# First down projection of a decoder trunk on one Trainium2 core: nine pairs of inner tiles as block products and four plain tiles

## The chip, the cores and the metric

The kernel is one program on one core of a Trainium2 chip. The metric is the device time of one execution, in microseconds (us). Names used below: PE (TensorE, the matmuls) and PEld (its weight loads), DVE (VectorE), ACT (ScalarE), POOL (GpSimd) and SP (SyncE). POOL and SP start DMAs here, each in the order of its own instruction stream; an instruction of any engine that waits for a semaphore holds up all that stands behind it on that engine. "Landing" is the moment at which a DMA's semaphore tells that its data are there.

## The reference, cut to what matters

The reference is one decoder layer on x of 512 x 1024, in float32, with a SwiGLU before and one behind a mixer:

```python
def swiglu(x, w_gate, w_up, w_down):
    return (jax.nn.silu(x @ w_gate) * (x @ w_up)) @ w_down
...
    x = x + 0.5 * swiglu(rmsnorm(x, ffn1_norm[l]), ffn1_wg[l], ffn1_wu[l], ffn1_wd[l])
    x = x + hybrid_mixer(...)
    x = x + 0.5 * swiglu(rmsnorm(x, ffn2_norm[l]), ffn2_wg[l], ffn2_wu[l], ffn2_wd[l])
```

The change is in the last product of the first line, h @ ffn1_wd: h is 512 x 2816 and ffn1_wd is 2816 x 1024. The inner size of 2816 makes 22 inner tiles of 128.

## The kernel before, in words

Every float32 product is made of three matmuls on rounded parts (fp32r): each operand is split into a rounded part and a remainder, and high x high, high x remainder and remainder x high are summed in PSUM. The rounding of a weight tile is an ACT instruction (`wh<-...`), its remainder a DVE subtraction (`wl<-...`, which reads `wh`). The function wsplit (line 242) does both.

**Stage U, the first up projection** (ffn_up, line 426, called at line 1082 with w1u) makes the 22 tiles of h; its last stretch is a stream of steps (p, w), block products of the weights of tile pair w, w from 0 to 15. Per w, three partial sums of weights are needed. They are kept in SBUF tiles: s1 and s3 are loaded by SP and completed by a POOL DMA that adds a second block as it lands (accum_op=ALU.add); s2 is made by DVE (s1 plus a block) and, for most w, turned into s4 by one more POOL DMA that adds the block a12 into the same tile. In the trace all of these POOL DMAs read `s<-w1u`. The last step of the stream is (3, 15): it uses the s4 of w = 15.

**Stage D, the first down projection** (block_down, line 821, with plain = PLAIN1 and pairs = PAIRS1) takes the 22 tiles of h in two ways:

- A plain tile k has two steps ("D", half, k), one for each half of the 1024 output columns. Each step is 4 x 3 matmuls of 512 columns. Its h tile is split into hh and hl (function halve, during stage U).
- A pair j of inner tiles, a(j) and b(j), has seven steps (p, j), p = 1 to 7: block products in place of the eight block multiplications of a plain 2 x 2 scheme (Strassen's scheme, in a form with few additions). Each step is 4 x 3 matmuls of 256 columns. The seven weight operands are a11, a12, a22 and the sums s1 = a21 + a22, s2 = s1 + a11, s3 = a11 + a21 (with the signs of the scheme held by the other side) and s4 = s2 + a12. The seven moving operands are tiles cm of 128 x 512, a rounded half and a remainder half, made of a(j), b(j) and differences of them: `cr<-h,h` and `h<-h` are the two DVE subtractions of function differences (line 882), and operand (line 900) makes the rounded half on ACT and the remainder on DVE (or, for p = 4, by a POOL DMA).

The order of work in stage D is a list, `steps`. Before, it is 6 plain steps of half 0; then p = 1, 2, 5 for all j; then p = 6 and 3, with four plain steps of half 1 among them; then p = 7; two plain steps; and p = 4: 68 steps. What each step needs is hung on a table of tasks by step number (function task), and the tasks of step i are issued right after the matmuls of step i: the split of step i's weights at i - 4, most operands at i - 5 or i - 6, the differences of pair j at step j, the operand of (7, j) at j + 1. Tasks with negative numbers are issued in the last steps of stage U (parameter ahead of ffn_up), in program order behind what that step issued itself. A finished chain of products is added into x by four DVE instructions (results1, `x<-aux,x` after the plain steps of half 0, `x<-mm,x` after p = 1).

The sums s1, s2 and s4 of a pair are made one after the other in one SBUF tile, sums[j] (trace name `sm`; there are eight such tiles, two buffers of 2048 columns), by an SP load and three POOL DMAs with addition, while the steps that use the earlier sum run. s3 is made beforehand in a DRAM tensor, `kept` (trace name `scr`), by two POOL DMAs (lines 976 and 977), and is loaded by SP thirteen steps ahead of its use.

The weights of a step are split into a third of a rotating set of buffers: wh and wl have three buffers of 1024 columns (tile pool wsp), so two steps share one, and the splits run at most six steps ahead of PE.

The class Blocks (line 322) exists already for the second feed-forward layer: it owns four DRAM tensors for one pair's s1 to s4, and stages() returns six groups of DMAs, in which each group needs the landing of the one before: SP copies a21 into s1 and s3; POOL adds a22 and a11 to them; POOL copies s1 into s2; adds a11; copies s2 into s4; adds a12.

Of the kernel before, what the change touches and what calls it, by code (L numbers as in the profile page):

```python
# [9 lines left out]
F32 = mybir.dt.float32  # L10
# [4 lines left out]
P = 128  # L15
S = 512
D = 1024
# [25 lines left out]
HS = S // 2  # L43
TAIL2 = 4
LEAD = 4
PLAIN1, PAIRS1, PAIRS2, TAIL = 6, 8, 11, 3
DIRECT1, DIRECT2 = 4, 4
SUMS_AHEAD = 3
UNITS, SUMS_FROM, SUMS_PART, DIRECT_PART, SUMS_STEPS, SUMS_TIME = 6, 37, 0.93, 0.04, 44, 142
# [130 lines left out]
def hybrid_kernel(ctx, tc, xt, vec, w1u, w1d, wm, wki, wrg, watt, wrnn, wout, w2u, w2d, gf, out):  # L180
# [4 lines left out]
    Q = plan.engine("SP", nc.sync)  # L185
# [17 lines left out]
    def nm(s):  # L203
        cnt[0] += 1
        return f"{s}_{cnt[0]}"

    def slot(dt=F32, name="s"):
        return plan.take("slot", big.tile([P, S], dt, tag="slot", name=nm(name)))
# [612 lines left out]
    def block_down(hs, wd, sums, plain, pairs, blocks=None):  # L821
# [7 lines left out]
        steps = [("D", 0, k) for k in range(plain)] + [(p, j) for p in (1, 2, 5) for j in range(pairs)]  # L829
        for p in (6, 3):  # L830
            for j in range(pairs):
                steps += [(p, j)] + [("D", 1, (6, 3).index(p) * 2 + j // 3)] * (j in (2, 5) and plain > 2)
        steps += [(7, j) for j in range(pairs)] + [("D", 1, k) for k in range(plain - 2, plain)] + [(4, j) for j in range(pairs)]
        if blocks:
            steps = [(p, j) for p in (1, 2, 6, 5, 7, 3, 4) for j in range(pairs)]
# [3 lines left out]
        def task(i, *fs):  # L839
            tasks.setdefault(i, []).extend(fs)  # L840

        def block(b, j):

            i, half = b * (pairs // 2) + j // 2, j % 2 * S
            return wd[i][:, half:half + S]

        units, turned, ra, raws, s3 = {}, {}, {}, {}, {}

        def source(i):
            p, j = steps[i]  # L850
            b = blocks[j]
            return {1: b.a11, 2: b.a12, 3: b.s4, 4: b.a22, 5: b.s1, 6: b.s2, 7: b.s3}[p]

        def load_pair(i):
            raws[i] = raw.tile([P, WMAX], F32, tag="raw", name=nm("wr"))
            for n in range(min(2, len(steps) - i)):
                Q.dma_start(raws[i][:, n * S:(n + 1) * S], source(i + n))

        def split_pair(i):
            units[i // 2] = [wsp.tile([P, WMAX], F32R, tag=t, name=nm(t)) for t in ("wh", "wl")]  # L860
            c = slice(0, min(2, len(steps) - i) * S)
            wsplit(*(t[:, c] for t in (raws.pop(i), *units[i // 2])))
# [8 lines left out]
        def unit(i, src):  # L871
            def split_():
                if i % 2 == 0:
                    units[i // 2] = [wsp.tile([P, WMAX], F32R, tag=t, name=nm(t)) for t in ("wh", "wl")]
                wsplit(src(), *(t[:, i % 2 * S:(i % 2 + 1) * S] for t in units[i // 2]))

            return split_

        a = lambda j: hs[plain + 2 * j]
        b = lambda j: hs[plain + 2 * j + 1]  # L880
# [54 lines left out]
            task(i - before, operand(p, j, p != 4))  # L935

        used = []
        assert blocks or len(steps) % 2 == 0
        for i, st in enumerate(steps):
            if blocks and i % 2 == 0:  # L940
                task(i - 4, lambda i=i: split_pair(i))
                task(i - 9, lambda i=i: load_pair(i))
            if blocks:
                moved_operand(i, *st)
                continue
            if st[0] == "D":
                _, h, k = st
                key = ("D", h, k // 2)
                if k % 2 == 0:
                    used.append([i - 4, index["D", h, k + 1] - 4, key, 2 * pairs + h * (plain // 2) + k // 2])  # L950
                task(i - 4, unit(i, lambda key=key, k=k: raws[key][:, k % 2 * S:(k % 2 + 1) * S]))
                continue
            p, j = st
            if p in (1, 4, 2):
                key = (p, j // 2)
                if j % 2 == 0:
                    used.append([i - 4, index[p, j + 1] - 4, key, {1: 0, 2: 1, 4: 3}[p] * (pairs // 2) + j // 2])
                src = lambda key=key, j=j: raws[key][:, j % 2 * S:(j % 2 + 1) * S]
            elif p == 7:
                src = lambda j=j: s3[j]  # L960
            else:
                src = lambda j=j: sums[j]
            if p == 5:
                def base(j=j):
                    Q.dma_start(sums[j], block(2, j))

                def add(j=j):
                    G.dma_start(sums[j], block(3, j), accum_op=ALU.add)

                task(3 * j // 2 + 2, base)  # L970
                task(3 * j // 2 + 4, add)
            if p == 7:
                kept = scr.tile([P, S], F32, name=nm("scr"))
                n = 0 if j < pairs // 2 else 1
                first_, then_ = ((j - 200, j - 199), (6 * j - 66, 6 * j - 59))[n]
                task(first_, lambda j=j, o=kept: nc.gpsimd.dma_start(o, block(2, j)))
                task(then_, lambda j=j, o=kept: nc.gpsimd.dma_start(o, block(0, j), accum_op=ALU.add))

                def fetch_sum(j=j, o=kept):
                    s3[j] = slot(F32, "s3")  # L980
                    Q.dma_start(s3[j], o)

                task(i - 13, fetch_sum)
            if p == 6:
                def third(j=j):
                    G.dma_start(sums[j], block(0, j), accum_op=ALU.add)

                task(index[5, j] - 3, third)
            if p == 3:
                def fourth(j=j):  # L990
                    G.dma_start(sums[j], block(1, j), accum_op=ALU.add)

                task(index[6, j] - 3, fourth)
            moved_operand(i, p, j)
            task(i - 4, unit(i, src))
# [83 lines left out]

    sums = []  # L1080
    d1 = block_down(hs, w1d, sums, PLAIN1, PAIRS1)
    ffn_up(y, w1u, 2, DIRECT1, hs, PLAIN1, V_G1, norm1, (-0.5, -0.4, -0.3, 0.3), ((WP[0], WP[1]), (WP[2], pu)), AH[1:], d1.tasks_at, wide=WIDE1)

# [104 lines left out]
    steps, index, last = d1.steps, d1.index, len(d1.steps) - TAIL  # L1188
# [70 lines left out]
    with tc.manual_schedule(engines=ENGINES):  # L1259
# [3 lines left out]
        for i in range(last):  # L1263
            if i == 0:
                for k in ("pth", "ptl"):
                    t = ptp.tile([P, NQ * S], F32, tag=k, name=nm("sm"))
# [642 lines left out]


    d2 = block_down(hs, w2d, x, 0, PAIRS2, BLOCKS2D)
    for m in range(NQ):
        for half in range(2):
            d2.tasks.setdefault(-80 + 8 * m + 4 * half, []).append(lambda m=m, half=half: Q.dma_start(
                rows(m, half), xrows[m * QB:(m + 1) * QB, half * S:(half + 1) * S]))
    steps, index, units, turned, tasks_at = d2.steps, d2.index, d2.units, d2.turned, d2.tasks_at
# [127 lines left out]
def _tiles(w, kt, m=P):  # L2044
    k, n = w.shape
    return w.reshape(kt, P, n // m, m).transpose(2, 1, 0, 3).reshape(n // m, P, kt * m)


def _cols(v):
    return v.reshape(-1, KD, P).transpose(2, 0, 1).reshape(P, -1)  # L2050


def _layout(i):
    def blocks(d, n, m):

        t = d[0].reshape(KF, P, 2, S)
        pairs = t[n:].reshape(m, 2, P, 2, S).transpose(3, 1, 0, 2, 4).reshape(2 * m, 2, P, S).transpose(0, 2, 1, 3).reshape(2 * m, P, 2 * S)
        plain = t[:n].reshape(n // 2, 2, P, 2, S).transpose(3, 0, 2, 1, 4).reshape(n, P, 2 * S)
        return np.concatenate([pairs, plain])

    turned = np.arange(D).reshape(NQ, KD, 32).transpose(1, 0, 2).reshape(-1)
    up = lambda g, u: np.stack([_tiles(g[0][turned], KD), _tiles(u[0][turned], KD)], axis=1)
    w = i["w_in"][0][turned]

    wa, wx = (i[g][0].reshape(KD, 2, 64, 64) for g in ("rg_wa", "rg_wx"))
    rg = np.concatenate([np.stack([wa[:, 0], wx[:, 1]], 1), np.stack([wx[:, 0], wa[:, 1]], 1)], axis=3).reshape(KD, P, P)
    bx = i["rg_bx"][0].reshape(KD, 2, 64)[:, ::-1].reshape(1, D)
    vec = np.concatenate(
        [_cols(i[n][:, turned]) for n in ("ffn1_norm", "mix_norm", "ffn2_norm")] + [_cols(i["final_norm"])]
        + [_cols(i["conv_w"][0]), _cols(i["conv_b"][0]), _cols(i["rg_ba"][0]), _cols(bx), _cols(i["rg_lam"][0])], axis=1)  # L2070
    return {
        "xt": i["x"][0].T[turned].reshape(KD, P, S),
        "vec": vec,
        "w1u": up(i["ffn1_wg"], i["ffn1_wu"]),
        "w1d": blocks(i["ffn1_wd"][:, :, turned], PLAIN1, PAIRS1),
        "wm": _tiles(np.concatenate([w[:, :896], w[:, 936:]], axis=1), KD),
        "wki": _tiles(w[:, 896:936], KD, 40)[0],
        "wrg": rg,
        "watt": _tiles(i["w_att_proj"][0], 4),
        "wrnn": _tiles(i["w_rnn_proj"][0], KD),  # L2080
        "wout": _tiles(i["w_out"][0][:, turned], KD),
        "w2u": up(i["ffn2_wg"], i["ffn2_wu"]),
        "w2d": blocks(i["ffn2_wd"], 0, PAIRS2),
        "gf": i["final_norm"].reshape(-1),
    }
# [14 lines left out]
```

## Time and profile before

| | |
|---|---|
| median of 3 runs | 1048.92 us (1048.9 to 1049.15) |
| the profiled execution | 1048.70 us, span 1046.9 us |
| granted TensorE clock of the profiled execution | 0.999 |
| PE busy | 1039.2 us, 99% of the span |
| DVE busy | 888.6 us, 85% |
| ACT busy | 666.5 us, 64% |
| POOL busy | 264.9 us, 25% |
| stage D, first to last matmul | from 231.44 us to 344.86 us |

The span runs from the first to the last instruction; 1.8 us of the profiled execution's time lie around it. In the rows of a timeline stand the start, the duration, the engine, the line of the code, the operation, the tile written and those read, and in brackets the idle time of the engine before it with what ended that. Most of the program's instructions are recorded through one helper and so carry one line, 174; the groups are told apart by the names of their tiles. Matmuls overlap: the time that one takes from PE is the distance from its start to the next one's start, not its duration. The same holds, to a smaller degree, for DVE and ACT, where a following instruction may start up to 0.1 us ahead of the end of the one before.

### The profile page before, as it was taken

The page shows a single profiled execution, that of the slowest core. Times are in us where ns is not written, and L with a number is a line of the kernel's source. Part 1 is how long each engine was busy: PE and PEld are TensorE (multiplying, and loading weights), DVE is VectorE, ACT ScalarE, POOL GpSimd, SP SyncE. Part 2 cuts the span into 40 slices and gives each one's busy share as a digit, 9 for nine tenths or more (in the row PEclk, how much of TensorE's full clock was granted, in tenths as well). Part 3 has the DMA queues.
Part 4 walks back from the last instruction along what each step waited for, and adds up shares of the span by engine and source line. Part 5 has one row for each costly group of instructions (what it writes and reads, how often), then busy time and mean ns, then how long its engine had stood idle before and what let it go on. Part 6 is the DMA issues. An engine that isn't in the chain of part 4 may idle for free.

```text
span 1046.9 us, 16653 instructions
## 1 busy us (share of the span) xinstructions
PE 1039.2 (99%) x5664; PEld 898.2 (86%) x5664; DVE 888.6 (85%) x1767; ACT 666.5 (64%) x1257; POOL 264.9 (25%) x390
## 2 busy tenths in 40 slices
PE   9999999999999999999999999999999999999997
PEld 8889999989999888888888888888899888888886
DVE  6679999989968789898999976785898788899896
ACT  7466666655657557797956574344666666667765
POOL 0261223302524012332200454554630000001100
PEclk9999999999999999999999999999999999999999
DMA  9686998948998579888833888989983666557784
GB/s 331 163 163 172 267 237 219 230 113 230 249 236 187 161 194 235 215 219 221 214 101 101 222 199 222 301 228 331 255 219 74 202 225 206 193 174 202 237 234 149
DMA packets 100870, 218.12 MB, mean 208 GB/s; under 512 B 12624, under 2 KB 19920, under 8 KB 100048
## 3 DMA queue, kind: packets, MB, share of 16 engines
q1 hardware_dynamic: 63168, 140.57, 40.3%
q0 software_dynamic: 37184, 76.04, 36.9%
q8 instruction: 44, 0.72, 0.3%
q10 hardware_dynamic: 432, 0.44, 0.1%
q14 instruction: 42, 0.34, 0.1%
HBM read 204.95 MB, written 56.62 MB: 250 GB/s over the span
## 4 chain that ended last, share of the span: by engine, by line
PE 99%; DVE 0%; ACT 0%; issue 0%; ACTq 0%
PE mm L174 71%; PE aux L174 28%; DVE o L174 0%; DVE x L174 0%; ACT sq L174 0%; ACT ss L174 0%; DVE sq L174 0%; DVE rs L174 0%; DVE ss L174 0%; DVE mean L174 0%; DVE epst L174 0%; ACTq L174 0%
## 5 line engine op out<-in xcount | busy, mean ns | idle before, releaser
L174 DVE TENSOR_TENSOR wl<-wr,wh 128x1024 fp32r<-128x1024 f32 (+2 forms) x238 | 237.7, 1003 | 56.7 <-ACT wh L174 53.7
L174 ACT ACTIVATE wh<-wr 128x1024 fp32r<-128x1024 f32 (+3 forms) x239 | 208.2, 876 | 80.2 <-PE mm L174 28.8
L174 PE MATMUL mm<-cm,wh 128*128 128x256 f32 (+1 forms) x1184 | 240.9, 310 | 0.0
L174 PEld LDWEIGHTS mm<-cm,wh 128*128 128x128 f32 x1184 | 189.4, 191 | 7.5 <-ACT tu L174 0.2
L174 PE MATMUL mm<-cm,wl 128*128 128x256 f32 x736 | 172.5, 282 | 0.0
L174 PE MATMUL mm<-yh,wh 128*128 128x512 f32 (+1 forms) x416 | 164.7, 396 | 0.0
L174 PE MATMUL mm<-yl,wh 128*128 128x512 f32 (+1 forms) x416 | 162.5, 391 | 0.0
L174 PE MATMUL mm<-yh,wl 128*128 128x512 f32 x408 | 159.3, 390 | 0.0
L174 PEld LDWEIGHTS mm<-cm,wl 128*128 128x128 f32 x736 | 130.0, 190 | 6.1
L174 PE MATMUL aux<-cm,wh 128*128 128x512 f32 (+1 forms) x472 | 122.9, 379 | 0.0
L174 PEld LDWEIGHTS mm<-yh,wh 128*128 128x128 f32 (+1 forms) x416 | 78.2, 188 | 17.6 <-issue 1.4
L174 PEld LDWEIGHTS mm<-yl,wh 128*128 128x128 f32 (+1 forms) x416 | 77.7, 187 | 15.3 <-DVE yl L174 0.3
L174 PEld LDWEIGHTS mm<-yh,wl 128*128 128x128 f32 x408 | 76.7, 188 | 16.3
L174 PEld LDWEIGHTS aux<-cm,wh 128*128 128x128 f32 x472 | 79.7, 189 | 9.4
L174 ACT ACTIVATE wh<-s 128x512 fp32r<-128x512 f32 x96 | 58.8, 626 | 44.0 <-DVE s L174 32.7
L174 PE MATMUL mm<-wh,cm 128*128 128x512 f32 x264 | 81.4, 389 | 0.0
L174 DVE TENSOR_TENSOR wl<-s,wh 128x512 fp32r<-128x512 f32 x96 | 65.4, 688 | 15.1 <-ACT wh L174 14.5
L174 PEld LDWEIGHTS aux<-cm,wl 128*128 128x128 f32 x440 | 68.8, 189 | 8.7
L174 PE MATMUL aux<-cm,wl 128*128 128x256 f32 x440 | 74.0, 281 | 0.0
L330 POOL DMA_DIRECT2D scr<-w2d x44 | 42.1, 1086 | 117.7 <-DMA scr<-w2d 104.7
L162 POOL DMA_DIRECT2D s<-w1u x44 | 41.4, 1141 | 115.1 <-DVE wl L174 70.5
L162 POOL DMA_DIRECT2D cm<-h x20 | 17.3, 864 | 203.6 <-ACT cm L174 159.9
(263 smaller groups left out, 2106.6 us busy)
## 6 DMA issues: line engine op xcount, KB each, us to landing
wr<-scr SPq DMA_DIRECT2D x92, 256.0 KB, 3.1
wr<-wm SPq DMA_DIRECT2D x39, 512.0 KB, 4.4
scr<-w2u POOLq DMA_DIRECT2D x72, 256.0 KB, 6.9
scr<-scr POOLq DMA_DIRECT2D x46, 256.0 KB, 7.1
s<-w1u POOLq DMA_DIRECT2D x44, 256.0 KB, 7.5
scr<-w2d POOLq DMA_DIRECT2D x44, 256.0 KB, 6.8
wr<-w1u SPq DMA_DIRECT2D x19, 512.0 KB, 6.3
wr<-w1d SPq DMA_DIRECT2D x18, 512.0 KB, 4.6
```

What stands on the lines that cost most here:

```text
L162: return self.engine.dma_start(out, src, **kw)
L174: return call(*args, **kw)
L330: plain, adds = nc.gpsimd.dma_start, lambda o, i: nc.gpsimd.dma_start(o, i, accum_op=ALU.add)
```

## The change

Nine of the eleven pairs of inner tiles go by block products, not eight, and four inner tiles stay plain, not six. Stage D has 4 + 27 + 18 + 2 + 9 + 2 + 9 = 71 steps: four plain steps at the start, p = 1, 2 and 5 for nine pairs, p = 6 with two plain steps of half 1 among them, p = 3, p = 7, two plain steps, p = 4.

There are only eight SBUF tiles for sums. So the sums of two pairs, j = 7 and j = 8 (FORMED1), are made in DRAM by Blocks.stages() ahead of stage D, at the tasks 3n + j - 27 for the groups n = 0 to 5, that is from -20 to -4, in the last twenty steps of stage U. Their steps with p = 5, 6, 3 and 7 load the finished sum from DRAM by SP into a tile s3, thirteen steps ahead. Pair 8 has no partner with which to share a 1024-column load, so its steps with p = 1, 2 and 4 also load single blocks in this way, and the layout of w1d in DRAM is arranged for that. Pairs 0 to 6 keep their sums in SBUF and their s3 in `kept`, at the same task numbers as before. The s3 of pair 7, which had two POOL DMAs at the tasks -24 and -17, goes into its Blocks.

```diff
-PLAIN1, PAIRS1, PAIRS2, TAIL = 6, 8, 11, 3
+PLAIN1, PAIRS1, FORMED1, PAIRS2, TAIL = 4, 9, (7, 8), 11, 3
...
-                steps += [(p, j)] + [("D", 1, (6, 3).index(p) * 2 + j // 3)] * (j in (2, 5) and plain > 2)
+                steps += [(p, j)] + [("D", 1, j // 3)] * (j in (2, 5) and p == 6)
...
+        if not blocks:
+            formed = {j: Blocks(*(block(b, j) for b in range(4))) for j in FORMED1}
+            for j, o in formed.items():
+                for n, moves in enumerate(o.stages()):
+                    task(3 * n + j - 27, *(lambda m=m: m[0](m[1], m[2]) for m in moves))
...
+            if j in formed and (p in (5, 6, 3, 7) or j == pairs // 2 * 2):
+                def fetch_formed(i=i):
+                    s3[i] = slot(F32, "s3")
+                    Q.dma_start(s3[i], source(i, formed))
+
+                task(i - 13, fetch_formed)
+                moved_operand(i, p, j)
+                task(i - 4, unit(i, lambda i=i: s3[i]))
+                continue
```

Two places in the order of the instructions matter below.

The first is POOL's stream at the end of stage U. The s names are the SBUF tiles of the up projection: s2_415 and s2_418 are the s4 of w = 14, s2_432 and s2_435 that of w = 15. scr is a DRAM tensor of stage D, sm the SBUF sums. Before:

```order
L977 DMA scr_49_353<-w1d 128x512
L162 DMA s1_411_2459<-w1u 128x512
L162 DMA s3_412_2460<-w1u 128x512
L162 DMA s2_415_2490<-w1u 128x512
L977 DMA scr_50_354<-w1d 128x512
L162 DMA s2_432_2603<-w1u 128x512
L162 DMA sm_548_2871<-w1d 128x512 x4
```

After (scr_43, scr_44 and scr_46 are s1, s2 and s4 of pair 7, scr_45 its s3; scr_47 to scr_50 are those of pair 8):

```order
L162 DMA s2_418_2492<-w1u 128x512
L330 DMA scr_43_347<-w1d 128x512
L330 DMA scr_45_349<-w1d 128x512
L330 DMA scr_47_351<-w1d 128x512
L330 DMA scr_49_353<-w1d 128x512
L851 DMA scr_44_348<-scr_43_347 16x4096
L851 DMA scr_48_352<-scr_47_351 16x4096
L330 DMA scr_44_348<-w1d 128x512
L162 DMA s2_435_2610<-w1u 128x512
L330 DMA scr_48_352<-w1d 128x512
L851 DMA scr_46_350<-scr_44_348 16x4096
L851 DMA scr_50_354<-scr_48_352 16x4096
```

Between the s4 of w = 14 and that of w = 15 stood one DMA; now seven stand there, of which the copy into scr_44 needs the landing of the addition to scr_43, and the addition to scr_44 the landing of that copy.

The second is DVE's stream during p = 1 of stage D. x0 to x3 are the four additions after the plain steps of half 0; cr and h are the differences of one pair; cm are remainders of moving operands; wl remainders of weights. Before, from these additions to the differences of the last pair:

```order
L174 SCALAR_TENSOR_TENSOR x0_88<-aux_550_2873,x0_88 128x512
L174 SCALAR_TENSOR_TENSOR x1_89<-aux_551_2877,x1_89 128x512
L174 SCALAR_TENSOR_TENSOR x2_90<-aux_552_2881,x2_90 128x512
L174 SCALAR_TENSOR_TENSOR x3_91<-aux_557_2904,x3_91 128x512
L174 TENSOR_TENSOR wl_580_3045<-wr_560_2921,wh_579_3044 128x512
L174 TENSOR_TENSOR cr_581_3048<-h_431_2601,h_419_2526 128x256
L174 TENSOR_TENSOR h_431_2601<-h_431_2601 128x256
L174 SCALAR_TENSOR_TENSOR cm_582_3051<-h_431_2601,cm_582_3051 128x256
L174 TENSOR_TENSOR cm_583_3055<-cr_571_2990,cm_583_3055 128x256
L174 TENSOR_TENSOR wl_580_3045<-wr_560_2921,wh_579_3044 128x512
L174 TENSOR_TENSOR cr_581_3048<-h_455_2773,h_450_2733 128x256
L174 TENSOR_TENSOR h_455_2773<-h_455_2773 128x256
```

After, the same additions and what follows them:

```order
L174 SCALAR_TENSOR_TENSOR x0_88<-aux_556_2894,x0_88 128x512
L174 SCALAR_TENSOR_TENSOR x1_89<-aux_557_2898,x1_89 128x512
L174 SCALAR_TENSOR_TENSOR x2_90<-aux_558_2902,x2_90 128x512
L174 SCALAR_TENSOR_TENSOR x3_91<-aux_563_2925,x3_91 128x512
L174 TENSOR_TENSOR cr_576_3011<-h_324_1888,h_306_1799 128x256
L174 TENSOR_TENSOR h_324_1888<-h_324_1888 128x256
L174 TENSOR_TENSOR wl_578_3015<-wr_460_2790,wh_577_3014 128x512
L174 SCALAR_TENSOR_TENSOR cm_579_3018<-h_400_2369,cm_579_3018 128x256
L174 TENSOR_TENSOR cm_580_3022<-cr_567_2956,cm_580_3022 128x256
L174 TENSOR_TENSOR cr_576_3011<-h_362_2127,h_346_2041 128x256
L174 TENSOR_TENSOR h_362_2127<-h_362_2127 128x256
L174 TENSOR_TENSOR wl_578_3015<-wr_460_2790,wh_577_3014 128x512
```

Three more pairs of differences follow these rows, up to h_461 of the last pair: behind the four additions DVE now makes the differences of five pairs (j = 4 to 8), before of two (j = 6 and 7). The additions themselves now stand behind the weights of step 7, before behind those of step 9.

More of the change, by code (lines that the diff above doesn't have):

```diff
@@ L842, in block, with source @@
         def block(b, j):
-            i, half = b * (pairs // 2) + j // 2, j % 2 * S
+            i, half = (b * (pairs // 2) + j // 2, j % 2 * S) if j < pairs // 2 * 2 else (2 * pairs - 2 + b // 2, b % 2 * S)
             return wd[i][:, half:half + S]
+        if not blocks:
[3 more added lines that the diff above has]
+                    task(3 * n + j - 27, *(lambda m=m: m[0](m[1], m[2]) for m in moves))
         units, turned, ra, raws, s3 = {}, {}, {}, {}, {}
-        def source(i):
+        def source(i, blocks=blocks):
             p, j = steps[i]
@@ L937, in block_down @@
         used = []
-        assert blocks or len(steps) % 2 == 0
         for i, st in enumerate(steps):
@@ L959, in block_down @@
             elif p == 7:
-                src = lambda j=j: s3[j]
+                src = lambda i=i: s3[i]
             else:
@@ L977, in block_down, with fetch_sum @@
                 task(then_, lambda j=j, o=kept: nc.gpsimd.dma_start(o, block(0, j), accum_op=ALU.add))
-                def fetch_sum(j=j, o=kept):
-                    s3[j] = slot(F32, "s3")
-                    Q.dma_start(s3[j], o)
+                def fetch_sum(i=i, o=kept):
+                    s3[i] = slot(F32, "s3")
+                    Q.dma_start(s3[i], o)
                 task(i - 13, fetch_sum)
@@ L2056, in blocks @@
         t = d[0].reshape(KF, P, 2, S)
-        pairs = t[n:].reshape(m, 2, P, 2, S).transpose(3, 1, 0, 2, 4).reshape(2 * m, 2, P, S).transpose(0, 2, 1, 3).reshape(2 * m, P, 2 * S)
+        own = m // 2 * 2 if n else m
+        rows = lambda v: v.reshape(-1, 2, P, 2, S).transpose(3, 1, 0, 2, 4).reshape(-1, 2, P, S).transpose(0, 2, 1, 3).reshape(-1, P, 2 * S)
+        pairs = np.concatenate([rows(v) for v in (t[n:n + 2 * own], t[n + 2 * own:]) if len(v)])
         plain = t[:n].reshape(n // 2, 2, P, 2, S).transpose(3, 0, 2, 1, 4).reshape(n, P, 2 * S)
```

## The prediction

> **What bounds the kernel now.** I read the page's shares, its clock row and its chain of waits first.
>
> ```profile
> PE 1039.2 (99%) x5664; PEld 898.2 (86%) x5664; DVE 888.6 (85%) x1767; ACT 666.5 (64%) x1257; POOL 264.9 (25%) x390
> ...
> PEclk9999999999999999999999999999999999999999
> ...
> PE 99%; DVE 0%; ACT 0%; issue 0%; ACTq 0%
> ```
>
> PE is busy throughout, at an undisturbed clock, and the chain that ends last is PE from end to end. So matmul work taken out comes off the end, and every stall put into PE is added to it. The second question is how near to PE the engines that feed it run. The table of windows answers it for the end of stage U, the plain steps of half 0 (231.44 to 247.81), p = 1 (to 259.32) and p = 5 to 7 with the plain steps among them. Its columns are the stretch, its length, the busy time of PE, PEld, DVE, ACT and POOL, the granted clock, the share of the DMA engines and GB/s.
>
> ```profile
> 181.00:215.00 34.00, 34.00 (x222) 30.95 (x222) 30.71 (x58) 21.46 (x46) 13.38 (x17) 1.00 1.01 233
> 215.00:219.00 4.00, 4.00 (x29) 3.70 (x28) 3.68 (x8) 1.86 (x5) 0.00 (x0) 1.00 0.01 2
> 231.44:247.81 16.37, 16.37 (x74) 13.52 (x73) 14.63 (x36) 7.14 (x18) 2.61 (x3) 1.00 0.75 200
> 247.81:259.32 11.51, 11.51 (x97) 11.51 (x96) 11.24 (x34) 9.16 (x21) 1.32 (x2) 1.00 0.86 243
> 282.36:344.86 62.50, 62.50 (x458) 59.58 (x457) 47.54 (x98) 38.34 (x83) 22.50 (x32) 1.00 0.88 209
> ```
>
> PE has no idle time in any of them. In p = 1 DVE is busy for 11.24 of 11.51 us: no room is left. The DMA engines are full up to 215 and empty just after it. These two rows decide the case.
>
> **PE's part: a gain of 0.84 us.** The timeline of PE gives both kinds of step from starts (0.40 is a duration and overlaps the next).
>
> ```profile
> 229.68 0.40 PE L174 MATMUL mm<-cm,wh 128*128 128x256 f32 x2
> 229.92 0.28 PE L174 MATMUL mm<-cm,wl 128*128 128x256 f32 x1
> 230.04 1.09 PE L174 MATMUL aux<-cm,wh 128*128 128x512 f32 x4
> ...
> 231.44 0.40 PE L174 MATMUL aux<-hh,wh 128*128 128x512 f32 x1
> ...
> 247.81 0.40 PE L174 MATMUL mm<-cm,wh 128*128 128x256 f32 x2
> ...
> 259.32 0.40 PE L174 MATMUL aux<-cm,wh 128*128 128x256 f32 x2
> ```
>
> Six plain steps take 247.81 - 231.44 = 16.37 us, 2.73 each; the eight steps of p = 1 take 11.51, 1.44 each. Two plain tiles fewer are four plain steps, 10.91 us; a ninth pair is seven block steps, 10.07 us. The difference is -0.84 us.
>
> **DVE's part: 1.2 us too late in p = 2.** Two plain steps of half 0 less are 5.46 us less time ahead of p = 1, in which DVE made differences and weight remainders in advance; and a ninth pair's differences and operands come in. I walk DVE's new order with the distances from start to start in the old timeline.
>
> ```profile
> 226.17 0.69 DVE L174 TENSOR_TENSOR wl<-s,wh 128x512 fp32r<-128x512 f32 x1 [0.97 <-ACT wh L174]
> ...
> 227.83 0.42 DVE L174 TENSOR_TENSOR tu<-aux,tu 128x256 f32<-128x256 f32 x1 [0.36 <-ACT tu L174]
> ...
> 231.78 0.69 DVE L174 TENSOR_TENSOR wl<-wr,wh 128x512 fp32r<-128x512 f32 x1 [0.28 <-ACT wh L174]
> ...
> 234.38 0.42 DVE L174 TENSOR_TENSOR cr<-h,h 128x256 f32<-128x256 f32 x1
> ...
> 247.20 2.48 DVE L174 SCALAR_TENSOR_TENSOR x<-aux,x 128x512 f32<-128x512 f32 x4
> 249.59 0.68 DVE L174 TENSOR_TENSOR wl<-wr,wh 128x512 fp32r<-128x512 f32 x1
> 250.19 0.42 DVE L174 TENSOR_TENSOR cr<-h,h 128x256 f32<-128x256 f32 x1
> 250.64 0.43 DVE L174 TENSOR_TENSOR h<-h 128x256 f32<-128x256 f32 x1
> 250.99 0.42 DVE L174 SCALAR_TENSOR_TENSOR cm<-h,cm 128x256 fp32r<-128x256 f32 x1
> 251.32 0.42 DVE L174 TENSOR_TENSOR cm<-cr,cm 128x256 fp32r<-128x256 f32 x1
> ...
> 254.66 0.17 DVE L174 TENSOR_SCALAR zt<-zt 128x8 f32<-128x8 f32 x1
> ...
> 255.40 0.68 DVE L174 TENSOR_TENSOR wl<-wr,wh 128x512 fp32r<-128x512 f32 x1
> ...
> 256.33 0.16 DVE L174 TENSOR_TENSOR cc<-cc,zt 128x8 f32<-128x8 f32 x1
> ...
> 256.63 0.69 DVE L174 TENSOR_TENSOR wl<-wr,wh 128x512 fp32r<-128x512 f32 x1
> ...
> 261.53 1.41 DVE L174 SCALAR_TENSOR_TENSOR x<-mm,x 128x256 f32<-128x256 f32 x4
> 262.85 0.68 DVE L174 TENSOR_TENSOR wl<-wr,wh 128x512 fp32r<-128x512 f32 x1
> ```
>
> The prices: a weight remainder 0.60, a pair's two differences 0.80, an operand remainder 0.335, four additions into x 2.39 (512 wide) or 1.32 (256 wide), a zt group 0.74, a cc pair 0.30. The first difference, at 234.38, loses one weight remainder ahead of it and gains one operand: 234.12. Up to the additions into x then stand four weight remainders, four pairs of differences and seven operands: 2.40 + 3.20 + 2.35 = 7.95, so the additions start at 242.07 (PE leaves the four plain steps at 242.35, and they read its four results one by one, so they cost little more) and end at 244.46. From there to the weights of step 17, which is (2, 4): five pairs of differences 4.00, ten weight remainders 6.00, fourteen operands 4.69, zt 0.74, four cc pairs 1.20, the additions of p = 1 1.32, together 17.95. The last weight remainder is out at 262.41, and 0.08 later as its duration outlasts its distance: 262.5. PE reaches step 17 after four plain and thirteen block steps, at 231.44 + 10.91 + 18.70 = 261.05, and needs the remainder at the third matmul, 0.24 later by the first two PE rows: 261.3. DVE is **1.2 us late**. In the old program the same weights were out at 263.53 (the row at 262.85) and PE was there at 259.32 + 4 x 1.44 = 265.07, so DVE was 1.5 us ahead. Behind it a step asks DVE for a remainder, an operand and a cc pair, 1.24 against PE's 1.44, so DVE catches up, but a stall once taken stays.
>
> **POOL's part: the s4 of w = 15 lands late.** These are POOL's rows, ACT's reader of that sum, and the landing times: first that of the L977 addition, second that of the s4 of w = 15, then two groups of DMAs with their size and median time to landing, SP's loads of stage D's weights (200 to 230) and POOL's DRAM copies (316 to 345).
>
> ```profile
> 209.28 0.86 POOL L162 DMA_DIRECT2D s<-w1u  x1 [5.01 <-DVE wl L174]
> 209.82 1.18 POOL L977 DMA_DIRECT2D scr<-w1d  x1
> 219.96 0.88 POOL L162 DMA_DIRECT2D s<-w1u  x1 [8.96 <-DVE wl L174]
> ```
>
> ```profile
> 225.51 0.62 ACT L174 ACTIVATE wh<-s 128x512 fp32r<-128x512 f32 x1
> ```
>
> ```profile
> DMA to landing us min/median/max: 5.8/5.8/5.8
> ```
>
> ```profile
> DMA to landing us min/median/max: 4.0/4.0/4.0
> ```
>
> ```profile
> wr<-w1d SPq DMA_DIRECT2D x3, 512.0 KB, 3.4
> ```
>
> ```profile
> scr<-scr POOLq DMA_DIRECT2D x3, 256.0 KB, 3.0
> ```
>
> Before, this DMA left at 219.96 and landed at 223.94; ACT used it at 225.51, DVE 0.66 later, PE in (3, 15) at 230.04. Now it stands behind the sums of pairs 7 and 8: the copy into scr_44 holds POOL until the addition to scr_43 has landed, the addition to scr_44 until that copy has.
>
> No trace shows this chain, so it goes by bounds. The addition to scr_43 leaves in the place of the L977 row, 209.82. Short end: it takes 4.0 and the copy 3.0, over at 216.8, ahead of 219.96: nothing is late. Long end: the addition takes 5.8 (215.6), and the engines, full until 215, are given three transfers of 256 KB more than before (four SP copies of a21 come, one leaves); at 233 GB/s each takes 1.1, 3.4 in all. I take half, 1.7, for what lies ahead of the addition: 217.3. The copy leaves then, but three further additions are queued (3.3, to 220.6), the copy itself takes 1.1 and half a 512 KB load of SP 1.1: 222.8, where the row of 3.0 alone would say 220.3. I take the later one, since the rows from full engines are nearer. The addition to scr_44 and the s4 leave together: 5.8 and 1.1 more make **T = 229.7** for its landing, 231.4 with the whole 3.4.
>
> ACT and DVE work in order, and the splits of stage D stand behind that sum. DVE's remainder moves from 226.17 to T + 0.66; the idle 0.36 and 0.28 up to 231.78 take up 0.64 of that, but a new operand fills 0.34 of them. DVE's whole walk shifts by T - 225.81, here 3.9 us, and PE's stall in p = 2 grows by it. PE's direct wait, in (3, 15) for the rounded half at T + 0.7 against 230.04, is a part of that stall and not added.
>
> **The rest at nothing.** The step weights of pairs 7 and 8 come by SP thirteen steps (19 us) ahead, against 3.4 for twice the bytes. The SBUF sums of pairs 0 to 6 keep their task numbers, with three POOL additions fewer. In p = 5 to 7 DVE has 15 us to spare in 62.5 and ACT 24; were that cover gone, each 1 us would cost 1 us.
>
> **The sum.** -0.84 + 1.2 + 3.9 = +4.3 us. The profiled execution took 1048.70 (span 1046.9 and 1.8 around it), 0.22 under the median, which changes nothing here: **1053.0 us**.
>
> **The rivals.**
>
> *Only DVE is late.* The sums in DRAM finish early, T stays below 225.8, and what remains is -0.84 + 1.2 = +0.4: 1049.1 us, not slower by a measurable amount. This is the case on the other side. For it: the window after 215 shows idle DMA engines, and the short end is over 3 us before 219.96. Against it: the 5.8 us row, taken where the chain starts. Deciding point: the s4 of w = 15 leaves by 221.8. The Trainium skill ("DMA: Bandwidth & Descriptors", "Anatomy of one DMA — SWDGE (gpsimd) path") fits a POOL DMA as about 2.0 us plus its bytes at 436 GB/s, 2.6 us for 256 KB as an estimate; by it the two steps would be over at 215.0 and this rival would hold. The trace disagrees: 5.8 and 4.0 us for additions, 3.0 for a plain copy.
>
> *Nothing waits.* DVE makes up its 1.2 us too, if its distances shrink by 0.02 us over some 70 instructions or if PE stalls elsewhere unseen. Then the full gain comes: 1047.9 us. The row with 0.27 us of DVE idle in p = 1 speaks against it.
>
> *The sum is far later.* With each chained DMA at 5.8 us behind the full backlog, T is 234, PE stands still at the end of stage U, and 234 - 225.81 + 1.2 - 0.84 = +8.5: 1057.2 us.
>
> **How the numbers follow.** My forecast, both waits, gets 0.60; only DVE late 0.22; nothing waits 0.13; far later 0.05. The forecast's own range is T from 227.5 to 231.4, +2.0 to +6.0. The range for 8 in 10 reaches from the full gain, 1047.8, to 1055.0; what is outside is the forecast's upper edge, the far case and little below. About 0.2%, 2.1 us, is what a measurement of this kernel can tell from no change. Slower: 0.53 of the forecast and 0.05, 0.58. Same: 0.07 of the forecast's low edge, 0.22, and 0.10 of "nothing waits", 0.39. Faster needs more than the full PE gain: 0.03.
>
> **What would show it.** Right: the last issue of s<-w1u on POOL at about 222.8 in place of 219.96, ACT's and DVE's rows for it near 230 with idle time ended by that DMA, and weight loads of PE idle behind DVE's wl in p = 1 and 2, 5 us in all. Only DVE late: that issue near 220 and about 1 us of waits at steps 16 to 18. Wrong altogether: PE without gaps through p = 2, or stalls from p = 5 on, where I count on spare time.

## The result, and the profile after

The changed kernel takes 1054.26 us (median of six runs, 1053.35 to 1055.36) against 1048.91 us before (1048.5 to 1049.2): ratio 1.0051, 95% interval 1.0038 to 1.0064. The profiled execution is the fastest of the six, 1053.35 us with a span of 1051.6, 4.65 us above the profiled execution of before.

The page of after, in the lines that answer to those of before:

```profile
PE 1040.3 (99%) x5700; PEld 899.2 (86%) x5700; DVE 892.7 (85%) x1778; ACT 669.5 (64%) x1266; POOL 270.2 (26%) x398
...
PEclk9999999999999999999999999999999999999999
...
PE 90%; DVE 4%; issue 2%; DMA 1%; POOL 1%; ACT 0%; DVEq 0%; POOLq 0%; ACTq 0%
```

The shares still say "99% PE". The third line says more: the chain that ended last is no longer PE from end to end. 4% of it are now DVE's, and POOL and a DMA stand in it. Where these lie, the waits of PE between 200 and 350 us say (engine, what it was about to write, who released it; then us in total, times, the longest):

```profile
PE mm L174 <- ACT tu L174: 2.1, 1, 2.1
PE aux L174 <- DVE wl L174: 0.7, 2, 0.4
PE mm L174 <- DVE wl L174: 0.4, 1, 0.4
```

Before, the same view has no row at all. The windows of after put the waits into their stages; stage D starts at 233.83, p = 1 at 244.75, p = 2 at 258.79 and p = 5 at 273.08:

```profile
215.00:219.00 4.00, 4.00 (x29) 3.70 (x28) 3.69 (x8) 1.85 (x5) 0.52 (x1) 1.00 1.02 167
...
224.00:233.83 9.83, 7.71 (x52) 6.82 (x51) 4.66 (x10) 3.54 (x8) 4.07 (x6) 1.00 0.72 135
233.83:244.75 10.92, 10.92 (x50) 9.01 (x49) 10.71 (x26) 6.03 (x14) 0.83 (x1) 1.00 0.89 249
244.75:258.79 14.04, 13.62 (x109) 13.09 (x108) 13.77 (x37) 10.41 (x25) 3.49 (x4) 1.00 0.90 228
258.79:273.08 14.29, 13.58 (x110) 13.12 (x109) 13.94 (x49) 8.40 (x20) 2.94 (x4) 1.00 0.98 276
```

The columns are those of the prediction's table. Read PE's busy time, the second number behind the stretch, against DVE's, the fourth. From 224 to 233.83 PE works 7.71 of 9.83 us: 2.1 are lost at the end of stage U, with DVE idle for half of the time, so DVE isn't the cause there. In p = 1 and p = 2 PE loses again, and there DVE is busy nearly throughout. The first row shows the DMA engines full (1.02) in the four microseconds in which they stood empty before. Stage D's ends are these rows of PE:

```profile
233.83 0.40 PE L174 MATMUL aux<-hh,wh 128*128 128x512 f32 x1
...
348.82 0.40 PE L174 MATMUL mm<-yh,wh 128*128 128x512 f32 x1
```

Before, stage D began at 231.44 and ended at 344.86, 113.42 us. Now it begins 2.39 us later and takes 114.99, 1.57 more, although its matmuls are 0.84 shorter: 2.41 us are lost in it, counted from start to start (the view of waits lists 1.1 of them, since it counts only the time behind the recorded ends, which overlap the next starts). By its end 3.96 us are lost; the other 0.7 come later: 0.44 between 990 and 1003, in the second down projection, to which e3_both comes back, and 0.25 behind the last matmul.

Why the end of stage U stalls stands in three short timelines. POOL:

```profile
209.82 3.71 POOL L330 DMA_DIRECT2D scr<-w1d  x4
218.36 0.52 POOL L851 DMA_DIRECT2D scr<-scr  x1 [4.83 <-DMA scr<-w1d]
220.94 0.50 POOL L851 DMA_DIRECT2D scr<-scr  x1 [2.05 <-DMA scr<-w1d]
223.56 0.84 POOL L330 DMA_DIRECT2D scr<-w1d  x1 [2.12 <-DMA scr<-scr]
224.10 1.22 POOL L162 DMA_DIRECT2D s<-w1u  x1
```

ACT:

```profile
225.23 0.39 ACT L174 ACTIVATE tu<-mm 128x256 f32<-128x256 f32 x1 [0.50 <-DVE mm L174]
229.42 0.63 ACT L174 ACTIVATE wh<-s 128x512 fp32r<-128x512 f32 x1 [3.80 <-DMA s<-w1u]
229.96 0.61 ACT L174 ACTIVATE wh<-wr 128x512 fp32r<-128x512 f32 x1
230.48 0.36 ACT L174 ACTIVATE tu<-mm 128x256 f32<-128x256 f32 x1
```

PE:

```profile
230.89 0.50 PE L174 MATMUL mm<-cm,wh 128*128 128x256 f32 x2 [2.12 <-ACT tu L174]
```

POOL waits for the landing of the additions (4.83 and 2.05), then for that of the first copy (2.12); only then the s4 of w = 15 leaves, at 224.10 instead of 219.96, and it lands 5.3 us later. ACT has nothing it is allowed to do until then: its idle 3.80 is ended by that DMA. What PE misses is not the rounded half itself but the `tu<-mm` two rows behind it, which reads out a PSUM bank that step (4, 15), the last but one of stage U, writes next. Before, PE reached this place at the same time, and the same instruction ran as soon as PE released it:

```profile
227.41 0.38 ACT L174 ACTIVATE tu<-mm 128x256 f32<-128x256 f32 x1 [0.75 <-PE mm L174]
```

After, it stood in line for 230.48 - 227.41 = 3.1 us behind one that could not run.

### The profile page after: what moved, and what is told of

Same layout as the page of the kernel before. It is cut to its first block, busy times and chain, and to the rows that moved or that the text cites. A ratio compares the mean times of both kernels' runs of the same rounds, so it can differ in the third digit from the quotient of the medians.

```text
span 1051.6 us, 16777 instructions
## 1 busy us (share of the span) xinstructions
PE 1040.3 (99%) x5700; PEld 899.2 (86%) x5700; DVE 892.7 (85%) x1778; ACT 669.5 (64%) x1266; POOL 270.2 (26%) x398
## 4 chain that ended last, share of the span: by engine, by line
PE 90%; DVE 4%; issue 2%; DMA 1%; POOL 1%; ACT 0%; DVEq 0%; POOLq 0%; ACTq 0%
PE mm L174 67%; PE aux L174 24%; DVE wl L174 2%; DMA scr<-w1d 1%; DVE cm L174 1%; DVE x L174 1%; DVE h L174 1%; POOL s L162 1%; DMA s<-w1u 1%; DVE cr L174 0%; ACT wh L174 0%; POOL scr L991 0%; DVE tu L174 0%; DVE o L174 0%; POOL scr L330 0%
## 5 line engine op out<-in xcount | busy, mean ns | idle before, releaser
L174 DVE TENSOR_TENSOR wl<-wr,wh 128x1024 fp32r<-128x1024 f32 (+2 forms) x234 | 235.0, 1008 | 57.1 <-ACT wh L174 52.6
L174 ACT ACTIVATE wh<-wr 128x1024 fp32r<-128x1024 f32 (+3 forms) x235 | 205.6, 880 | 77.4 <-PE mm L174 25.5
L174 PE MATMUL mm<-cm,wh 128*128 128x256 f32 (+1 forms) x1232 | 249.6, 309 | 2.1 <-ACT tu L174 2.1
L174 PEld LDWEIGHTS mm<-cm,wh 128*128 128x128 f32 x1232 | 196.7, 191 | 9.6 <-ACT tu L174 2.5
L174 PE MATMUL mm<-cm,wl 128*128 128x256 f32 x760 | 179.6, 282 | 0.4 <-DVE wl L174 0.4
L174 PEld LDWEIGHTS mm<-cm,wl 128*128 128x128 f32 x760 | 134.6, 190 | 7.1 <-DVE wl L174 0.8
L174 ACT ACTIVATE wh<-s 128x512 fp32r<-128x512 f32 x106 | 65.0, 625 | 48.0 <-DVE s L174 32.7
L174 DVE TENSOR_TENSOR wl<-s,wh 128x512 fp32r<-128x512 f32 x106 | 72.3, 688 | 19.9 <-ACT wh L174 19.0
```

The source lines that it names most:

```text
L174: return call(*args, **kw)
```

## The experiments

Theory A is the prediction's: the order on POOL makes the s4 late, the late s4 shifts DVE's walk, and DVE alone is a good microsecond late in p = 2. Rival B: DVE's order accounts for all of it and the s4 is absorbed. Rival C: the added traffic costs time, in whatever order it is issued. Runs of one group share the chip and the runs of before.

**e1_s4_first.** The copies and later additions behind the s4.

```diff
-task(3 * n + j - 27, *(...))
+task(3 * n + j - (27 if n < 2 else 22), *(...))
```

> The changed kernel with one move on POOL: the copies and later additions of the sums of pairs 7 and 8 (groups 2 to 5 of each) stand five steps later, behind the s4 of w = 15; all transfers stay. Theory A (the order on POOL makes the s4 late by 5 us, and DVE alone is 1.2 us late): the s4 leaves at 220 and lands between 224 and 225.8, PE stands nowhere before stage D, about 1.1 us of stalls stay in p = 2, and the time is that of the kernel before plus 1.1 less 0.84, 1049.2 us. Rival B (DVE's order alone is late by all of it, and the late s4 is absorbed): no change from the changed kernel, 1054.3. Rival C (the added traffic slows everything, in whatever order it is issued): no change either, 1053 to 1055.

Measured: 1050.45 us against 1049.03, ratio 1.0013 (1.0004 to 1.0022), eleven runs from 1049.45 to 1052.02. POOL's rows:

```profile
209.58 3.71 POOL L330 DMA_DIRECT2D scr<-w1d  x4
219.72 0.89 POOL L162 DMA_DIRECT2D s<-w1u  x1 [6.43 <-DVE wl L174]
220.28 1.35 POOL L851 DMA_DIRECT2D scr<-scr  x2
```

PE's waits from 200 to 350, all of them:

```profile
PE aux L174 <- DVE wl L174: 0.7, 2, 0.4
```

The wait for `tu` is gone and only DVE's in p = 2 is left, as A says; B and C fall as explanations of the whole. The profiled execution (1049.45) fits A's 1049.2; the median lies 1.2 us above it, which A doesn't explain.

**e2_decay_late.** The opposite half: POOL as in the change, less DVE work in p = 2.

```diff
-            if i > 6:
+            if i > 22:
                 next(cs, None)
```

> The changed kernel with the small zt and cc instructions (1.94 us of DVE ahead of the weights of step 17) put sixteen steps later, into p = 5; POOL as in the changed kernel. Theory A: the walk of DVE is still shifted by 3.6 us, and the tightest place is now step 12, 257.45 less 254.10 = 3.35 us late instead of 4.7 at step 17, so the time falls by 1.3 us to 1052.9, with 2.4 us of the stall still ahead of stage D. Rival B: DVE's lateness falls by the whole 1.94, to 1052.3, and the stall ahead of stage D is not affected by anything. Rival C: no change.

Measured: 1053.12 us against 1049.03, 1.0035 (1.0021 to 1.0049). PE's waits:

```profile
PE mm L174 <- ACT tu L174: 2.7, 1, 2.7
PE mm L174 <- DVE wl L174: 0.4, 1, 0.4
```

Four runs from 1050.65 to 1054.13: the time alone does not separate e2 from the change, whose interval it overlaps. The rows do.

The second row is the tell-tale: PE now waits for DVE in an `mm` step, so in p = 1, and nowhere in p = 2 (`aux`). The bound moved from step 17 to steps 10 to 12, as the walk said, and the stall at the end of stage U stayed. The profiled execution is the slowest of the four; by the starts of its matmuls it loses another 2.1 us between 980 and 1005.

**e3_both.** Both edits.

> Both moves: the s4 of w = 15 ahead of the copies, and zt and cc in p = 5. Theory A: no stall is left and the full gain of PE's work comes, 0.84 us under the kernel before: 1048.1 us. Rival B: 1052.3, as without the move on POOL. Rival C: 1053 to 1055.

Measured: 1049.08 us against 1049.03, 1.0003 (0.9995 to 1.0012), eleven runs from 1048.44 to 1051.19. No PE wait is listed between 200 and 350. The gain of 0.84 arrives at the end of stage D and is missing at the end of the program. In the second down projection (960 to 1005) the profile has these waits, the first of PE's weight loads, the second of ACT:

```profile
PEld mm L174 <- DVE wl L174: 1.5, 3, 0.6
```

```profile
ACT wh L174 <- DMA wr<-scr: 11.6, 7, 3.4
```

Before, ACT's is 9.8 us in six waits, the longest 2.5, and PEld has none.

**e4_chain_in_before.** The kernel before, with the twelve moves of the sums of two pairs added and nobody reading them.

```diff
+if not blocks:
+    spare = {j: Blocks(*(block(b, j) for b in range(4))) for j in (6, 7)}
+    for j, o in spare.items():
+        for n, moves in enumerate(o.stages()):
+            task(3 * n + j - 26, *(lambda m=m: m[0](m[1], m[2]) for m in moves))
```

> The kernel before with nothing but twelve more tasks: the sums of its pairs 6 and 7 are also made in DRAM, at the same step numbers as in the change, and nobody reads them (8 transfers more and the waits on POOL, no other edit). Theory A: the s4 of w = 15 leaves at 224 instead of 220 and lands at about 229.4; PE waits 2.4 us ahead of stage D as in the changed kernel; DVE is shifted by 3.2 us, of which its 1.8 us of spare time in p = 2 take a part, so that no more than these 2.4 us is lost: 1051.3 us. Rival B: 1048.9, since DVE's order is the old one. Rival C: 1052 or more, and stalls also where the s4 plays no part.

Measured: 1053.67 us against 1049.03, 1.0047 (1.0031 to 1.0064), five runs from 1050.8 to 1056.6, 2.4 more than A expected. In its profile (1056.36) the s4 left at 226.26, landed 5.9 us later, and PE's rows are:

```profile
228.22 0.63 PE L174 MATMUL aux<-cm,wl 128*128 128x256 f32 x4
233.69 0.80 PE L174 MATMUL mm<-cm,wh 128*128 128x256 f32 x2 [4.84 <-ACT tu L174]
...
238.80 0.39 PE L174 MATMUL aux<-hh,wh 128*128 128x512 f32 x1
```

The place and the releaser are those of the change, without its other edits: the chain on POOL alone slows the old kernel. By its median e4 would fit rival C too (1052 or more), but C also expected stalls elsewhere, and the view of PE's waits from 200 to 350 lists this one alone. The size was off twice. The s4 left 2.2 us later than in the change; an addition of the old kernel to its own kept sums stands among the first ones here, which would make the chain longer, though no run shows that this is the reason. And PE pays more than the wait: see the windows (the clock is the last number but two):

```profile
228.90:233.69 4.79, 0.00 (x0) 0.00 (x0) 0.81 (x2) 1.47 (x4) 0.52 (x1) 0.79 0.88 174
233.69:236.00 2.31, 2.31 (x11) 2.31 (x12) 2.24 (x6) 0.99 (x2) 1.36 (x2) 0.50 0.39 121
236.00:238.50 2.50, 2.50 (x9) 2.11 (x9) 2.19 (x6) 1.24 (x3) 0.83 (x1) 0.50 0.88 72
238.50:242.00 3.50, 3.50 (x19) 2.93 (x17) 3.16 (x8) 2.10 (x5) 0.00 (x0) 0.99 1.03 289
```

After the idle 4.8 us the granted clock is 0.50 for about 5 us. The two steps ahead of stage D take 238.80 - 233.69 = 5.11 us, where in the change they take 233.83 - 230.89 = 2.94: 2.2 us more. The five runs spread as their clocks do: 1050.8 at a mean granted clock of 0.999, close to A's 1051.3, and 1056.4 and 1056.6 at 0.995.

**e5_dram_shift, e6_both_gains_late, e7_before_gains_late** look for the microsecond that e1 and e3 leave.

The first edit is e5's, in the kernel before; the second is e6's in e3_both and e7's in the kernel before.

```diff
-    xrows = scr.tile([S, D], F32, name="xrows")
+    xrows = scr.tile([S + 384, D], F32, name="xrows")
```

```diff
-            if i == 24:
+            if i == 32:
                 gains()
```

> The kernel before with one DRAM tensor made longer by 1.57 MB, which nobody uses: all DRAM tensors behind it lie as far on as they do in the changed kernel (six sums more), and nothing else differs. The runs with the s4 first left 1 us more than the theory gives in each, and their profiles show it near the end, at 978 to 1000 us, where ACT waits for loads from such tensors. If the addresses do it: 1049.5 to 1050.5 with a wide spread. If not: 1049.0 as before.

> The kernel of e3_both with one more move, in the second down projection: the two broadcast loads of the last gains (gb) leave eight steps later, behind four pairs of weight loads instead of ahead of them. If what was left in e3_both is the wait of ACT for these weight loads near 980 us: the theory's full gain, 1048.1 us, and a narrower spread. If it lies elsewhere: 1049.1 as e3_both.

> The kernel before with only that move of gb. Its profile shows no stall of PE near 980 us, but its runs spread over 1.6 us. If that spread is the same wait: 1048.6 us. If the wait belongs to the changed kernels alone: 1049.0, no change.

Measured, against 1048.83: e5 1048.78, 0.9998 (0.9989 to 1.0007); e6 1048.39, 0.9997 (0.9988 to 1.0006), from 1047.81 to 1049.89; e7 1048.80, 0.9997 (0.9988 to 1.0006). The addresses do nothing. Moving gb does nothing for the kernel before, so its spread is something else. In e6 the best runs show the full gain, the others do not: its spread of 2.1 us is nearly as wide as that of e1 and e3 (2.6 and 2.8), so the wait near 980 us is not the whole of the missing microsecond.

**e8_s4_later.** One more copy ahead of the s4.

```diff
-task(3 * n + j - 27, *(...))
+task(3 * n + j - (27 if n < 2 else 30), *(...))
```

> The opposite of e1_s4_first: in the changed kernel groups 2 to 5 stand three steps earlier, so that the s4 of w = 15 stands behind the copy into scr_46 as well, which waits for the landing of the addition to scr_44. Theory A: the s4 leaves at about 228 and lands at about 233 instead of 229.4; PE's wait ahead of stage D grows from 2.1 to about 5.7 us, and since e4_chain_in_before showed PE at half clock behind a wait of 4.8 us, another 2.3 us is lost: about 3.5 to 4 us more than the changed kernel, 1058 us. Rival B: no change, 1054.3. Rival C: no change.

Measured: 1060.94 us against 1048.83, 1.0112 (1.0097 to 1.0128), 6.7 us above the change where A expected 3.7. POOL had one wait more than I had counted (the first copy now held up the additions behind it), the s4 left at 231.37 and landed 5.0 us later, and PE's wait is:

```profile
PE mm L174 <- ACT tu L174: 9.3, 1, 9.3
```

The wait grew by 7.2 us for 7.0 us of delay (236.4 against 229.4). The half clock behind it took about 2.3 us more (the two steps ahead of stage D take 5.29 us instead of 2.94), and the 2.41 us that the change lost in p = 1 and p = 2 are gone: DVE caught up while PE stood. B and C expected nothing.

**e9_all_behind_s4, e10_best.** The first four additions behind the s4 too; e10 has e6's two other edits besides.

```diff
-task(3 * n + j - 27, *(...))
+task(3 * n + j - (27 if n < 1 else 20), *(...))
```

> The changed kernel with groups 1 to 5 of the sums of pairs 7 and 8 behind the s4 of w = 15, the first four additions too (e1_s4_first left these ahead of it). There the s4 landed 4.8 to 5.8 us after its issue, at the very edge of what the splits can bear (225.8), and the median was 1.1 us above the theory's. If the s4 in a shared queue is what was left: it lands in about 4 us again, the runs draw together, and the time is that of the kernel before plus DVE's 1.1 less 0.84: 1049.1 us. If something else was left: 1050.2 to 1050.5 as e1_s4_first.

> The same with zt and cc in p = 5 and gb eight steps later: every stall that was found is taken away. Theory: the full gain of PE's work, 0.84 us under the kernel before, 1048.0 us, in most runs. If an eighth to a half of it goes missing as in e6_both_gains_late: 1048.4.

Measured, against 1049.10: e9 1051.76, 1.0031 (1.0019 to 1.0043); e10 1050.39, 1.0012 (1.0003 to 1.0021). Both expectations failed, in the direction of rival C. The s4 did land in 4 us again, and yet, each against its own runs of before, e9 is 1.2 us slower than e1, and e10 1.7 us slower than e6. PE's waits in e10 from 200 to 350:

```profile
PE aux L174 <- ACT wh L174: 1.0, 1, 1.0
PE aux L174 <- DVE wl L174: 0.5, 2, 0.2
```

ACT's rows that DMAs released, e10, from 250 on:

```profile
254.84 0.63 ACT L174 ACTIVATE wh<-wr 128x512 fp32r<-128x512 f32 x1 [0.62 <-DMA wr<-w1d]
...
260.64 0.63 ACT L174 ACTIVATE wh<-wr 128x512 fp32r<-128x512 f32 x1 [4.04 <-DMA wr<-w1d]
...
265.24 0.63 ACT L174 ACTIVATE wh<-wr 128x512 fp32r<-128x512 f32 x1 [2.84 <-DMA wr<-w1d]
```

The last two are the weights of steps 17 and 19, the loads for (2, 4) and (2, 6). Whatever is put behind the s4 is moved into 220 to 260, where SP's loads of stage D need the same DMA engines. In e3 ACT started on the first of these at 259.43, and PE did not wait for them. That e1, e3 and e6 paid a part of this price in their slower runs is possible, but not shown.

**e11_chain_spread, e12_spread_best.** So the sums are put where neither matters.

```diff
-task(3 * n + j - 27, *(...))
+task(14 * n + j - 116, *(...))
```

> The changed kernel with all six groups of the sums of pairs 7 and 8 spread over stage U, fourteen steps (some 20 us) apart, from about 75 to 180 us; nothing else. The s4 of w = 15 stands behind no copy, and none of these transfers is left for the stretch from 205 to 260. The runs with the sums behind the s4 showed a second price, the weights of steps 17 and 19 landing late in full DMA engines. If that and the place of the s4 are the whole of it, DVE's 1.1 us is all that stays: 1049.2 us. If the transfers cost as much wherever they are (rival C): 1050.5 or more, with PE idle in stage U.

> The same with zt and cc in p = 5 and gb eight steps later in the second down projection. Theory: no stall stays, 1048.0 us, with a spread no wider than that of the kernel before. Rival C: 1049.5 or more.

Measured, against 1049.07: e11 1050.30, 1.0011 (1.0003 to 1.0020); e12 1048.24, 0.9992 (0.9983 to 1.0001), eleven runs from 1047.81 to 1048.56, against 1048.33 to 1049.69 of before. e11 missed A's 1049.2 by 1.1 us and lies just under the 1050.5 of rival C; but C expected PE to stand idle in stage U, and from 7 us on no wait of PE is listed ahead of p = 2. PE in e11 and e12, stage D from start to end:

```profile
231.97 0.40 PE L174 MATMUL aux<-hh,wh 128*128 128x512 f32 x1
...
345.86 0.40 PE L174 MATMUL mm<-yh,wh 128*128 128x512 f32 x1
```

```profile
231.21 0.40 PE L174 MATMUL aux<-hh,wh 128*128 128x512 f32 x1
...
343.79 0.40 PE L174 MATMUL mm<-yh,wh 128*128 128x512 f32 x1
```

e11: 113.89 us, 0.47 more than before: -0.84 and 1.31 of DVE, whose waits in p = 2 are the only ones listed. e12: 112.58, 0.84 less than before, to the hundredth what the two kinds of steps said. e12 keeps all that the change computes and transfers; its median is under that of both kernels, by 0.8 us under the kernel before, though the interval still touches no difference.

## Why the prediction held, point by point

The forecast was 4.3 us more than before; measured are 5.35 by the medians and 4.65 by the profiled executions.

*PE's part, -0.84 us.* Right: stage D of e12 is 0.84 us shorter, with the same matmuls.

*DVE's part, 1.2 us.* Right: 1.31 in e11, where nothing else stalls in stage D. Instructions of one shape kept their distances here, so an order that was never run could be walked with them: the weights of step 17 were out 31.05 us after the start of stage D in e11, and 31.06 by the walk. The walk also had to be right about the place: in e2 the next tight one came up where its list had it.

*POOL's part, T = 229.7 and a shift of 3.9 us.* In the profiled execution T is 224.10 + 5.3 = 229.4, though the s4 left at 224.10 and not at the 222.8 named as the sign. DVE's remainder of the s4 starts at 230.08 instead of 226.17; less the 0.30 that idle time took up, its walk shifts by 3.6. Together -0.84 + 1.3 + 3.6 = 4.1 by the end of stage D; measured 3.96. The first addition landed 8.0 us after its issue instead of 7.5, the copy at 223.3 instead of 222.8, and the s4 then took 5.3 us instead of 6.9. The estimate had split its bounds by halves that no row gave, so that T came out this close is in part luck.

*PE's direct wait as a part of the stall and not added.* Right in size: 2.39 ahead of stage D and 2.41 in it make the one lateness of DVE. The place was wrong: I had named 5 us of waits in p = 1 and p = 2 as the sign, half of which came ahead of stage D, and PE stopped a step earlier than I had said, for the `tu` behind the rounding in ACT's line, not for the rounded half. I had listed the splits of stage D as what stands behind that wait on ACT, and left out the copies that free PSUM.

*The rest at nothing.* Right for p = 5 to 7, where no wait is listed. Wrong at the end: 0.7 us of the 4.65 come after stage D, which no term had. In e3 the second down projection's weights land late (its rows above); in the change PE's weight loads wait there for DVE's `wl` too (0.7 us), but ACT waits no longer for loads than before, so what makes DVE late in it is open. Up to the end of stage D the sum was 0.3 us too high, so that 1053.0 lies so close to the profiled 1053.35 is partly two errors that cancel.

*The rivals.* "Only DVE late" is what e11 makes of the kernel, "nothing waits" is e12, "far later" is, roughly, e8 (T = 236.4 there, 234 in the forecast). The fit of the Trainium skill ("DMA: Bandwidth & Descriptors", "Anatomy of one DMA — SWDGE (gpsimd) path"), which gave 2.6 us for 256 KB as an estimate and spoke for the first, was far from the 8.0, 4.9 and 5.3 us that the addition, the copy and the s4 took here.

*The spread.* The median is 0.9 above the profiled execution. The change, e1 to e4, e9 and e10 spread over 2 to 6 us, e12 over 0.75. For the change the granted clocks point to a reason: 0.999 in the two fastest runs (1053.35 and 1053.52), 0.998 at 1054.12 and 0.997 in the three above. Means of 0.997 and less were measured only in kernels that stall at the end of stage U (this one, e2, e4 and e8); all other runs have 0.998 or 0.999. So in the slower runs the stall was probably long enough to halve the clock, as in e4's profile. No such run of the change was profiled, so this is argued and not shown; and it leaves the spread of e1, e3, e9 and e10 unexplained.

*Open.* e11's median lies 2.1 us above e12's. Their profiles, 2.6 apart, place the difference: 0.76 is there at the first matmul of stage D (231.97 against 231.21) and arises in the first 6 us of the program, which no edit touches; 1.31 is DVE's in stage D; 0.5 comes between 980 and 1000, in the second down projection, where only e12 has gb later. e6 against e3 points to 0.7 for gb, e7 to nothing in the kernel before. Why loads beside gb are later in some kernels was not found.

## What to carry to other kernels

A DMA that waits for another's landing, put into an in-order queue, delays everything behind it; look up what stands behind it and who needs that soonest, before looking at the bytes. Transfers that are needed late belong where the DMA engines and the queue have room, which here was neither just ahead of the deadline of another (e4, e8) nor just behind it (e9, e10), but spread over the 100 us before. And a kernel that is 99% PE can hide a second engine at 98% in one stage: walk that engine's new order with the old distances, since a gain of 0.8 us is easily given back.

## What the runs showed of the hardware

A PE wait of 2.12 us left the granted clock at 1.00 (the change). In e4 PE stopped at 228.9: the clock is 1.00 up to 231.70, 0.51 in the 2.0 us of idle time behind that, 0.50 when PE goes on at 233.69, and 1.00 from 238.6, 4.9 us later. In e8 PE stopped at 228.6; the clock is 1.00 up to 233.40, 0.50 from there, and 1.00 from 243.7, 5.9 us after PE went on at 237.82. The Trainium skill ("TensorE: Matmul & The Clock Gate", "What's actually happening") says that the clock is halved after an idle window of about 3.4 us and restored after one that is busy as long; the rows agree in kind, but here the clock fell 2.8 and 4.8 us after PE stopped and came back 4.9 and 5.9 us after it went on. On top of the stall itself this cost 2.2 us in e4.

An addition of 256 KB in DRAM landed 5.8 us after its issue in the kernel before. In the change the first of four that were issued together at the same place landed after 8.0 us, and POOL went on 8.5 us after its issue. The price of a step of the chain depended here on what was queued with it.
